# Gates of the product-key layers computed slice by slice at set paces, weight splits moved to VectorE, and a lookup of all heads at once

## The chip, the core and the metric

The kernel runs on one core of a Trainium2 chip. The metric is the device time of one launch in microseconds. The engines of the core that matter here are TensorE (PE, matrix products; its weight loads are listed as PEld), VectorE (DVE), ScalarE (ACT), GpSimd (POOL) and SyncE (SP, which issues the loads of the weights). Each engine takes its own instructions in the order in which they stand in its queue, and waits where data or a free buffer is missing.

## What is computed

The program is one inference step of a decoder of two layers for 256 prompt positions and 8 sample positions, 264 tokens in all. Each layer has a mixer and then a product-key layer ("PEER"); the change lies wholly in the second. Cut to what matters, for each token x (1024 numbers):

```
q = (x @ w_q).reshape(blk, 8, 256)                       # 8 heads
s1, s2 = q[..., :128] . k1 , q[..., 128:] . k2           # 128 scores each
v1, i1 = top_k(s1, 16); v2, i2 = top_k(s2, 16)
cand = v1[..., :, None] + v2[..., None, :]               # 16 x 16 pairs
sv, pos = top_k(cand, 16)
idx = take(i1 * 128 + i2, pos)                           # 16 experts a head
gates = softmax(sv)
h = einsum('thkd,td->thk', u_tab[idx], x)
y = einsum('thk,thkd->td', gelu(h) * gates, v_tab[idx])
```

There are 16384 experts, 128 x 128: an expert's number is i1 * 128 + i2. `u_tab` and `v_tab` have one row of 1024 numbers for each.

## The kernel before

**Prompt tokens are computed densely.** For the 256 prompt tokens the kernel doesn't gather. It multiplies all of `u_tab` with the tokens, applies gelu, multiplies by a gate that is zero for all experts but the chosen ones, and multiplies by all of `v_tab`. The 128 blocks of 128 experts that share an i1 are cut into four slices of 32 blocks (`SLICE`). `up(s)` makes `S[s]`, gelu of the products, 128 x 32 x 256, and `down(s)` multiplies `S[s]` into the output accumulators `Y`. `S` has three buffers, so the stages run up 0, up 1, up 2, down 0, up 3, down 1, down 2, down 3.

**Weights are split.** Each block of weights (128 x 1024, f32) comes by DMA into `wr` (line 49), ACT rounds it to `wh` (line 51), and VectorE or GpSimd subtracts to get the low part `wl` (line 55); three products (lines 110 to 112) then stand for one in full precision. `Stream.prep` keeps three blocks ahead of the one in use; `wh` and `wl` have four buffers. The number beside a block says which engine splits it: n means that every n-th split of the run falls to GpSimd, 0 would mean none. `peer_blocks` gives these numbers by slice. In the down stages the gated `S` is split likewise, into `ah` by ACT (line 486) and `al` by VectorE (line 488).

**Gates.** `weigh(pair)` makes the gates of two slices. For 16 tokens at a time (t0) VectorE builds one-hot rows: `ohB` over the 128 values of i2 (2048 elements) and `ohG` over the i1 of both slices (64 columns, 1024 elements), line 453; it multiplies the second by the gate's high and low part (line 470). PE multiplies the two for each token, twice (`products`, line 434, groups of 16 matmuls of 64 columns), into a buffer `pgen`, and VectorE multiplies `S` by that (`apply`, line 443).

**What sets the order.** The order is written by hand: under `manual_schedule` each engine's queue follows the code. Work beside the large products is written as generators that `yield` a cost in microseconds. `Background.spend(us)`, called after each weight block, runs the first generator in the list until that budget is used; `finish` drains one. The budget `RU` of 1.0 a block drives the top-k (`topk_head`, `topk_pairs`) during up 0 and up 1. Up 2 spends 2.4 a block on `weigh((0, 1))`, down 0 and up 3 spend 1.5 on the samples (`gathered`), down 1 spends 2.4 on `weigh((2, 3))`, down 2 nothing. `settle`, called at the end of a stage, drains a gate pass and then splits the first part of the next slice.

**Lookup.** `topk_pairs` turns positions among candidates into indices: for each half of the tokens, each side s and each of the 8 heads, it compares against `iota16` (f32), multiplies by the indices and sums over 16 entries (lines 209, 211, 213).

**Samples.** The 8 sample tokens have only 16 x 8 x 8 experts in all; `gathered` finds them, fetches their rows in 16 gathers that GpSimd issues (line 385, two buffers `grow`), and VectorE multiplies each (lines 395 and 402).

## Time and profile before

| | us |
|---|---|
| median of 3 runs | 2337.83 (2336.58 to 2338.54) |
| profiled execution, own time | 2338.07 |
| its span, first to last instruction | 2336.4 |
| PE busy | 2157.9 (92%) |
| VectorE busy | 1657.3 (71%) |
| GpSimd busy | 1008.6 (43%) |
| ScalarE busy | 945.1 (40%) |
| mean granted clock of TensorE | 0.967 of 2.4 GHz |

The two product-key layers take the stretches from 170.5 to 1089 us (layer 0) and from 1402 to 2320 us (layer 1) of the span; the first 62 and 60 us of each are the projection to q, the rest the eight stages. Matrix products on PE are pipelined: a product of 256 columns lasts about 0.28 us in the record, but the next one starts about 0.12 us after it. So the start times, and the idle time ahead of a group, tell more than PE's busy share. The releaser behind an idle time is the instruction whose end let the waiting one go.

### The profile page before, as it was taken

Reading aid. Unit: us, or ns where it says so; the run is one execution under the profiler, and the core shown is the slowest. Engines: PE = TensorE matmul, PEld = TensorE weight load, DVE = VectorE, ACT = ScalarE, POOL = GpSimd, SP = SyncE. Lnnn points to the kernel's source line nnn. Section 1 sums busy time; section 2 is a strip of 40 time slices with the busy share of each in tenths; the row PEclk is TensorE's granted clock in tenths of the full one; section 3 lists DMA queues with packets and bytes.
Section 4 is the critical chain, followed back from the end, with each engine's and each line's share of the span. In section 5 each row is a group of like instructions: output and inputs, shape, how many; then the busy total and the mean of one; then the engine's idle time right before and its main releaser. Section 6 shows DMA issues by size and latency. Waiting matters only on the chain.

```text
span 2336.4 us, 44010 instructions
## 1 busy us (share of the span) xinstructions
PE 2157.9 (92%) x17885; PEld 2031.2 (87%) x17885; DVE 1657.3 (71%) x2862; ACT 945.1 (40%) x1390; POOL 1008.6 (43%) x695
## 2 busy tenths in 40 slices
PE   8699999789999779999999999999789999779998
PEld 6379999789999779999766799999789999779997
DVE  8945699998743995445888755789998653995444
ACT  2424454224444224444543444444224444223443
POOL 6714444564534453222445334444554543553221
PEclk9799999899999889999999999999899999989999
DMA  5025554434775334553346545555434775334553
GB/s 178 26 93 176 178 181 163 136 114 149 264 244 178 109 109 154 185 177 133 132 145 220 172 142 165 187 172 170 137 109 145 260 236 187 120 105 149 183 172 106
DMA packets 111659, 371.56 MB, mean 159 GB/s; under 512 B 13865, under 2 KB 17857, under 8 KB 111456
## 3 DMA queue, kind: packets, MB, share of 16 engines
q1 hardware_dynamic: 104400, 347.73, 44.6%
q0 software_dynamic: 5728, 19.95, 2.5%
q8 instruction: 140, 2.29, 0.4%
q10 hardware_dynamic: 1328, 1.07, 0.1%
q14 instruction: 63, 0.52, 0.1%
HBM read 356.52 MB, written 12.18 MB: 158 GB/s over the span
## 4 chain that ended last, share of the span: by engine, by line
PE 55%; DVE 37%; DMA 3%; issue 2%; ACT 2%; POOL 1%; SPq 0%; ACTq 0%; DVEq 0%; POOLq 0%
PE Y L110 7%; PE Y L111 7%; PE Y L112 7%; PE pmm L110 7%; PE pmm L111 7%; PE pmm L112 7%; DVE ohG L470 7%; DVE ohG L453 4%; PE pmm L128 4%; DVE ohB L453 4%; DVE wl L55 3%; DVE tkt L209 3%; DVE S L443 3%; DVE tkt L211 2%; DVE al L488 2%
## 5 line engine op out<-in xcount | busy, mean ns | idle before, releaser
L55 POOL TENSOR_TENSOR wl<-wr,wh 128x1024 fp32r<-128x1024 f32 x303 | 759.9, 2511 | 998.4 <-ACT wh L51 937.1
L51 ACT ACTIVATE wh<-wr 128x1024 fp32r<-128x1024 f32 x579 | 610.2, 1055 | 645.1 <-PE pmm L111 144.2
L110 PE MATMUL pmm<-xh,wh 128*128 128x256 f32 (+1 forms) x2456 | 709.9, 289 | 1.9 <-ACT S L421 0.8
L112 PE MATMUL pmm<-xh,wl 128*128 128x256 f32 (+1 forms) x2456 | 697.0, 284 | 9.0 <-DVE wl L55 6.0
L111 PE MATMUL pmm<-xl,wh 128*128 128x256 f32 (+1 forms) x2456 | 698.6, 284 | 1.4 <-DVE xl L647 1.0
L110 PE MATMUL Y<-ah,wh 128*128 128x256 f32 x2048 | 592.6, 289 | 0.0
L55 DVE TENSOR_TENSOR wl<-wr,wh 128x1024 fp32r<-128x1024 f32 x276 | 364.5, 1321 | 321.2 <-ACT wh L51 320.4
L111 PE MATMUL Y<-al,wh 128*128 128x256 f32 x2048 | 586.8, 287 | 3.0 <-DVE al L488 2.9
L112 PE MATMUL Y<-ah,wl 128*128 128x256 f32 x2048 | 585.7, 286 | 0.0
L112 PEld LDWEIGHTS pmm<-xh,wl 128*128 128x128 f32 x2456 | 470.1, 191 | 10.6 <-DVE wl L55 7.2
L110 PEld LDWEIGHTS pmm<-xh,wh 128*128 128x128 f32 x2456 | 470.3, 191 | 5.0 <-ACT S L421 1.0
L111 PEld LDWEIGHTS pmm<-xl,wh 128*128 128x128 f32 x2456 | 471.2, 192 | 2.7 <-DVE xl L647 2.2
L111 PEld LDWEIGHTS Y<-al,wh 128*128 128x128 f32 x2048 | 400.3, 195 | 4.1 <-DVE al L488 4.0
L110 PEld LDWEIGHTS Y<-ah,wh 128*128 128x128 f32 x2048 | 400.4, 196 | 0.1
L112 PEld LDWEIGHTS Y<-ah,wl 128*128 128x128 f32 x2048 | 399.9, 195 | 0.0
L488 DVE TENSOR_TENSOR al<-S,ah 128x512 fp32r<-128x512 f32 x128 | 108.3, 848 | 157.1 <-ACT ah L486 157.1
L470 DVE TENSOR_TENSOR ohG<-ohG,gT 128x1024 f16<-128x1024 f16 x128 | 181.4, 1417 | 2.3
L486 ACT ACTIVATE ah<-S 128x512 fp32r<-128x512 f32 x128 | 80.5, 629 | 240.8 <-PE Y L112 236.8
L434 PE MATMUL pgen<-ohG,ohB 128*128 128x64 f16 x2048 | 87.2, 199 | 96.2 <-DVE ohG L470 82.9
L421 ACT ACTIVATE S<-pmm 128x512 f32<-128x512 f32 x128 | 76.3, 596 | 231.3 <-PE pmm L112 230.9
L434 PEld LDWEIGHTS <-ohB 128*128 128x128 f16 x2048 | 72.0, 101 | 107.9 <-DVE ohG L470 76.8
L128 PE MATMUL pmm<-x,wl 128*128 128x264 f32 x512 | 124.9, 401 | 7.9 <-DMA wl<-in_wie 6.6
(446 smaller groups left out, 2362.2 us busy)
## 6 DMA issues: line engine op xcount, KB each, us to landing
wr<-in_ut SPq DMA_DIRECT2D x256, 512.0 KB, 3.4
wr<-in_v SPq DMA_DIRECT2D x256, 512.0 KB, 3.4
wr<-in_wq SPq DMA_DIRECT2D x32, 512.0 KB, 3.5
wl<-in_wio SPq DMA_DIRECT2D x22, 512.0 KB, 3.6
wr<-in_wio SPq DMA_DIRECT2D x19, 512.0 KB, 4.8
S<-in_ssd SPq DMA_DIRECT2D x32, 256.0 KB, 2.7
out_s_ssd<-S SPq DMA_DIRECT2D x32, 256.0 KB, 3.0
wr<-in_woo SPq DMA_DIRECT2D x16, 512.0 KB, 4.0
```

The source lines that it names most:

```text
L51: k.nc.scalar.activation(hi, w, AF.Copy)
L55: eng.tensor_tensor(lo, w, hi, op=ALU.subtract)
L110: mm(out, wh, xh, start=first, stop=False, skip_group_check=True)
L111: mm(out, wh, xl, start=False, stop=False, skip_group_check=True)
L112: mm(out, wl, xh, start=False, stop=last, skip_group_check=True)
L128: self.nc.tensor.matmul(p[:, :T], wl[:, ts(i, 128)], x[:, kt], start=kt == 0, stop=kt == nk - 1, skip_group_check=True)
L421: nc.scalar.activation(S[s][:, e2:e2 + 2], p.rearrange("p (e t) -> p e t", e=2), AF.Gelu_apprx_tanh)
L434: nc.tensor.matmul(p[:, t * n:(t + 1) * n], B[:, 8 * h + t], AG[:, 8 * h + t, g], start=g == 0 and t == 0, stop=g == 1 and t == 7, skip_gr ...
L453: V.tensor_tensor(cols(out), iotah[:, i:i + n].rearrange("p (o a b) -> p o a b", o=1, b=2) .to_broadcast([128, nt, n // 2, 2]), spread(iT[ ...
L470: V.tensor_tensor(cols(AG[:, :, g]), cols(AG[:, :, 0]), spread(gT[:, g, tt], n), op=ALU.mult)
L486: nc.scalar.activation(ah, v, AF.Copy)
L488: V.tensor_sub(al, v, ah)
```

## The change

It has four parts.

First, `weigh` takes one or two slices. It is called for slice 0 alone, then for slices 1 and 2 together, then for slice 3 alone. For one slice `ohG` has 32 columns (512 elements), and a group of products is 32 matmuls of 32 columns for 16 tokens; each pass still builds `ohB` for all tokens. The pass for slice 0 is put behind the top-k in the same list, so it begins in up 1, as soon as the top-k is through; that for slices 1 and 2 runs in down 0 and up 3, that for slice 3 in down 1 and down 2. The yields follow the number of slices, and the budgets a block become 1.15 (up 0 to up 2), 1.3, 1.55, 0.9 and 0.9.

Second, `peer_blocks` gives 0 for everything but slice 0 of the up blocks and slice 3 of the down blocks, where every third split stays with GpSimd.

Third, the samples get a list of their own (`slow`) with budgets of 0.4, 0.1, 0.1, 0.25 and 0.25 a block from up 2 to down 2, and a row's gather is written behind the use of the row two before it.

Fourth, the lookup handles all 8 heads in one instruction in half precision, and sums the 16 entries by halving.

```
-RU, RQ = 1.0, 1.0
+RU, RQ = 1.15, 1.0
...
-            oh = pool.tile([128, gs, 16, 16], BF, name="tkt")
-            for g in range(g0, g0 + gs):
-                nc.vector.tensor_tensor(oh[:P, g - g0], ab[:P, s, g, :, None]..., k.iota16..., op=ALU.is_equal)
-                nc.vector.tensor_tensor(oh[:P, g - g0], oh[:P, g - g0], ff[:P, g, s, None, :]..., op=ALU.mult)
-            nc.vector.tensor_reduce(res[:P, s, g0:g0 + gs, :], oh[:P], axis=AX.X, op=ALU.add)
-            yield 0.9 * gs
+        oh = pool.tile([128, n, 16], FP16, name="ohB" if G > 1 else "tkt", bufs=2 if G > 1 else 1)
+        nc.vector.tensor_tensor(two, ab[:P, s, :, None]..., k.iota16[:P]..., op=ALU.is_equal)
+        yield 0.14 * G
+        nc.vector.tensor_tensor(four, four, ff[:P, :, s, None]..., op=ALU.mult)
+        yield 0.14 * G
+        for m in (8, 4, 2):
+            nc.vector.tensor_tensor(oh[:P, :, 0:m], oh[:P, :, 0:m], oh[:P, :, m:2 * m], op=ALU.add)
+        nc.vector.tensor_tensor(res[:P, s]..., oh[:P, :, 0], oh[:P, :, 1], op=ALU.add)
+        yield 0.16 * G
...
             rows = [row("u", 0), row("u", 1)]
+            yield 1.0
             for i in range(16):
-                if i + 2 < 16:
-                    rows.append(row("u" if i + 2 < 8 else "v", (i + 2) % 8))
...
-                yield 2.6
+                if i + 2 < 16:
+                    rows.append(row("u" if i + 2 < 8 else "v", (i + 2) % 8))
+                yield 1.5
...
                     bg.spend(us)
+                    slow.spend(us2)
...
-            n, i0 = 2 * SLICE, pair[0] * SLICE
+            n, i0 = len(pair) * SLICE, pair[0] * SLICE
+            tb = 512 // n
...
-                yield 2.3
+                yield 1.3 + 0.75 * len(pair)
...
-                yield 1.8
+                yield 1.1 * len(pair)
...
+        w = weigh((0,))
+        bg.add(w)
         up(0, RU)
         up(1, RU)
         for g in routes:
             bg.finish(g)
+        slow.add(gathered())
-        w = weigh((0, 1))
+        up(2, RU, 0.4, settle(w, 0))
+        w = weigh((1, 2))
         bg.add(w)
-        up(2, 2.4, settle(w, 0))
-        bg.add(gathered())
-        down(0, 1.5)
-        up(3, 1.5, settle(None, 1))
-        while bg.q:
-            bg.step()
-        w = weigh((2, 3))
+        down(0, 1.3, 0.1)
+        up(3, 1.55, 0.1, settle(w, 1))
+        w = weigh((3,))
         bg.add(w)
-        down(1, 2.4, settle(w, 2))
-        down(2, 0, settle(None, 3))
+        down(1, 0.9, 0.25, settle(None, 2))
+        down(2, 0.9, 0.25, settle(w, 3))
+        while slow.q:
+            slow.step()
...
-    return (ups(0, 2) + ups(1, 2) + ups(2, 1) + downs(0, 3) + ups(3, 3) + downs(1, 1) + downs(2, 3) + downs(3, 3))
+    return (ups(0, 3) + ups(1, 0) + ups(2, 0) + downs(0, 0) + ups(3, 0) + downs(1, 0) + downs(2, 0) + downs(3, 3))
```

Where instructions come to stand is shown at three places of layer 0. The line numbers are each program's own; after the change the split is still line 55, `onehot` is line 462, the multiply by the gate 479, `apply` 452, `al` 497 and the gather 391.

GpSimd from the start of up 0 on, before (`wl` is a split, `grow` a gather of the samples' rows):

```order
L548 IOTA iotah 128x128
L55 TENSOR_TENSOR wl<-wr,wh 128x1024 x66
L385 DMA grow<-in_u,idx 128x1024 x3
L55 TENSOR_TENSOR wl<-wr,wh 128x1024
L385 DMA grow<-in_u,idx 128x1024
L55 TENSOR_TENSOR wl<-wr,wh 128x1024
L385 DMA grow<-in_u,idx 128x1024 x2
L55 TENSOR_TENSOR wl<-wr,wh 128x1024
L385 DMA grow<-in_u,idx 128x1024 x2
L55 TENSOR_TENSOR wl<-wr,wh 128x1024
```

and after, up to the first load of the next layer's mixer:

```order
L558 IOTA iotah 128x128
L55 TENSOR_TENSOR wl<-wr,wh 128x1024 x10
L391 DMA grow<-in_u,idx 128x1024 x8
L391 DMA grow<-in_v,idx 128x1024 x8
L55 TENSOR_TENSOR wl<-wr,wh 128x1024 x11
L1194 DMA oddpar<-in_odd 128x154
```

Before, 66 splits stand ahead of the gathers, one or more between most of them, and 64 behind; after, 10 stand ahead of all gathers and 11 behind, 10 of these in down 3.

VectorE in the middle of a gate pass, before (up 2, slices 0 and 1; two groups of 16 tokens):

```order
L453 TENSOR_TENSOR ohB<-iotah,iT 128x2048
L443 TENSOR_TENSOR S<-S,pgen 128x32x8 x2
L453 TENSOR_TENSOR ohG<-iotah,iT 128x16x64
L443 TENSOR_TENSOR S<-S,pgen 128x32x8 x2
L470 TENSOR_TENSOR ohG<-ohG,gT 128x16x64 x2
L453 TENSOR_TENSOR ohB<-iotah,iT 128x2048
L443 TENSOR_TENSOR S<-S,pgen 128x32x8 x2
L453 TENSOR_TENSOR ohG<-iotah,iT 128x16x64
L443 TENSOR_TENSOR S<-S,pgen 128x32x8 x2
L470 TENSOR_TENSOR ohG<-ohG,gT 128x16x64 x2
```

and after (down 0, slices 1 and 2; a little over one group):

```order
L55 TENSOR_TENSOR wl<-wr,wh 128x1024
L462 TENSOR_TENSOR ohB<-iotah,iT 128x2048
L452 TENSOR_TENSOR S<-S,pgen 128x32x8 x2
L462 TENSOR_TENSOR ohG<-iotah,iT 128x16x64
L55 TENSOR_TENSOR wl<-wr,wh 128x1024 x2
L452 TENSOR_TENSOR S<-S,pgen 128x32x8 x2
L479 TENSOR_TENSOR ohG<-ohG,gT 128x16x64 x2
L55 TENSOR_TENSOR wl<-wr,wh 128x1024 x2
L462 TENSOR_TENSOR ohB<-iotah,iT 128x2048
L452 TENSOR_TENSOR S<-S,pgen 128x32x8 x2
```

The gate operations of a group are the same, but the splits of the weight blocks, which stood with GpSimd, now stand between them.

VectorE at the index lookup of the first half of the tokens, in up 0, before (three operations a head):

```order
L55 TENSOR_TENSOR wl<-wr,wh 128x1024
L209 TENSOR_TENSOR tkt<-ohG,iota_72 128x256
L211 TENSOR_TENSOR tkt<-tkt,ohG 128x256
L213 TENSOR_REDUCE ohG<-tkt 128x16
L209 TENSOR_TENSOR tkt<-ohG,iota_72 128x256
L211 TENSOR_TENSOR tkt<-tkt,ohG 128x256
L213 TENSOR_REDUCE ohG<-tkt 128x16
L55 TENSOR_TENSOR wl<-wr,wh 128x1024
```

and after (one side s of all heads, and the start of the next):

```order
L210 TENSOR_TENSOR ohB<-ohG,iota_72 128x2048
L55 TENSOR_TENSOR wl<-wr,wh 128x1024
L215 TENSOR_TENSOR ohB<-ohB,ohG 128x2048
L55 TENSOR_TENSOR wl<-wr,wh 128x1024
L218 TENSOR_TENSOR ohB<-ohB 128x128x8
L218 TENSOR_TENSOR ohB<-ohB 128x128x4
L218 TENSOR_TENSOR ohB<-ohB 128x128x2
L219 TENSOR_TENSOR ohG<-ohB 128x128
```

The 16 triples of a half of the tokens have become two runs of six operations, with splits between the large ones.

## Rows read from the trace of the kernel before

**Rows 1.** Windows by stage: us, busy time (count) by engine, granted clock, DMA share, GB/s.
```profile
232.40:324.90 92.50, 92.50 (x771) 92.50 (x771) 72.10 (x266) 45.50 (x52) 38.48 (x16) 0.98 0.54 178
324.90:419.70 94.80, 92.17 (x774) 91.36 (x773) 89.90 (x174) 43.82 (x50) 41.22 (x17) 1.00 0.52 171
419.70:564.20 144.50, 119.38 (x1286) 116.17 (x1284) 130.78 (x144) 43.25 (x50) 82.36 (x32) 0.92 0.36 122
564.20:659.80 95.60, 94.77 (x787) 94.17 (x786) 69.37 (x116) 45.04 (x53) 44.39 (x26) 1.00 0.76 256
659.80:750.60 90.80, 90.80 (x769) 90.80 (x769) 28.39 (x23) 42.88 (x49) 30.22 (x13) 1.00 0.60 195
750.60:901.50 150.90, 121.92 (x1282) 118.55 (x1281) 137.38 (x147) 42.71 (x49) 78.08 (x31) 0.90 0.34 112
901.50:993.70 92.20, 92.20 (x771) 92.20 (x769) 37.12 (x37) 42.22 (x48) 25.67 (x11) 1.00 0.57 188
...
1552.40:1649.00 96.60, 92.27 (x774) 91.45 (x774) 90.11 (x173) 43.31 (x50) 44.40 (x17) 1.00 0.51 169
1649.00:1793.20 144.20, 118.43 (x1285) 115.21 (x1284) 131.14 (x148) 43.25 (x50) 80.09 (x31) 0.92 0.37 125
1793.20:1891.90 98.70, 96.11 (x787) 95.74 (x786) 70.94 (x115) 46.64 (x54) 48.17 (x27) 0.98 0.74 248
...
1982.80:2131.90 149.10, 119.94 (x1282) 116.85 (x1282) 135.37 (x147) 42.74 (x49) 79.69 (x31) 0.91 0.35 116
```

**Rows 2.** Groups by line on PE, gate products in up 2, then down 1: busy, mean, idle before.
```profile
L434 PE MATMUL pgen<-ohG,ohB 128*128 128x64 f16 x512 | 21.4, 197 | 19.2 <-DVE ohG L470 16.5 <-DVE S L443 2.6
...
L434 PE MATMUL pgen<-ohG,ohB 128*128 128x64 f16 x512 | 21.9, 200 | 27.8 <-DVE ohG L470 23.7 <-DVE S L443 4.0
```

**Rows 3.** Timeline in up 2 (start, us), then durations of two gate lines, layer 0.
```profile
506.08 2.72 POOL L55 TENSOR_TENSOR wl<-wr,wh 128x1024 fp32r<-128x1024 f32 x1 [1.22 <-ACT wh L51]
...
507.13 2.21 DVE L453 TENSOR_TENSOR ohG<-iotah,iT 128x1024 f16<-128x1024 f16 x1
...
L470 DVE TENSOR_TENSOR ohG<-ohG,gT x64: 675/693/2882, 433.6 to 886.1; 128x1024 f16<-128x1024 f16 x64
...
L453 DVE TENSOR_TENSOR ohB<-iotah,iT x32: 1210/1218/3424, 431.8 to 878.5; 128x2048 f16<-128x2048 f16 x32
L453 DVE TENSOR_TENSOR ohG<-iotah,iT x32: 676/2220/2887, 432.9 to 880.3; 128x1024 f16<-128x1024 f16 x32
```

**Rows 4.** Durations (ns min/median/max): VectorE splits of the run; low parts and applications of layer 0.
```profile
L55 DVE TENSOR_TENSOR wl<-wr,wh x276: 1205/1226/3426, 150.8 to 2304.7; 128x1024 fp32r<-128x1024 f32 x138
...
L488 DVE TENSOR_TENSOR al<-S,ah x64: 675/693/2918, 563.7 to 1077.0; 128x512 fp32r<-128x512 f32 x64
...
L443 DVE TENSOR_TENSOR S<-S,pgen x128: 404/407/420, 438.1 to 895.0; 128x256 f32<-128x256 f32 x128
```

**Rows 5.** Timeline of PE in up 2: one group of gate products and the next matmul.
```profile
478.60 0.64 PE L434 MATMUL pgen<-ohG,ohB 128*128 128x64 f16 x16
479.08 0.37 PE L110 MATMUL pmm<-xh,wh 128*128 128x256 f32 x1
```

**Rows 6.** Durations of the three operations of the index lookup, layer 0.
```profile
L209 DVE TENSOR_TENSOR tkt<-ohG,iota x32: 412/425/2624, 308.7 to 425.0; 128x256 bf16<-128x256 f32 x32
...
L211 DVE TENSOR_TENSOR tkt<-tkt,ohG x32: 424/425/2523, 309.2 to 427.1; 128x256 bf16<-128x256 bf16 x32
...
L213 DVE TENSOR_REDUCE ohG<-tkt x32: 419/420/421, 309.7 to 429.6; 128x16 f32<-128x256 bf16 x32
```

**Rows 7.** Waits (us in total, times, longest): the whole run, then up 1 of layer 0.
```profile
DVE wl L55 <- ACT wh L51: 320.4, 187, 5.3
...
DVE tkc L395 <- DMA grow<-in_u,idx: 19.0, 6, 4.5
...
DVE wl L55 <- ACT wh L51: 1.9, 1, 1.9
...
PE pmm L112 <- DVE wl L55: 1.7, 2, 1.0
```

## What I expected, before the result

> **What bounds the kernel now.** I read the windows by stage first. [rows 1] cuts the product-key layers into stages of 32 weight blocks; the change touches seven a layer (up 0, 1, 2, down 0, up 3, down 1, 2) and not down 3. Five of the seven take 91 to 99 us with PE busy for nearly all of it. Two don't: up 2 takes 144.5 and 144.2 us, down 1 150.9 and 149.1. The floors stand in the same rows: an up stage in which PE never idles takes 90.8 (up 3), a down stage 92.2 (down 2). In the two long stages VectorE is busy 130.8 of 144.5 and 137.4 of 150.9 us, and PE's granted clock is 0.92 and 0.90. So PE is the bound everywhere but there, and there it is VectorE.
>
> [rows 2] shows how PE loses the time: it sat idle 19.2 us ahead of the gate products of up 2 and 27.8 us ahead of those of down 1, nearly all of it for the tile `ohG` of line 470. For down 1 the account closes: 27.8 idle, 15.4 of gate products (32 groups of 16 at 0.48 us, [rows 5]), and a clock 10% short over 150.9 us, 15.1: 58.3 of the 58.7 us above the floor. For up 2 it is 19.2 + 15.4 + 11.6 = 46.2 of 53.7.
>
> Next: why VectorE is so full. [rows 3] is one place: GpSimd splits a weight block from 506.08 for 2.72 us, and a gate operation of VectorE that starts at 507.13 lasts 2.21 us, ending about half a microsecond after the split does. The same form takes 0.676 at its fastest; its median in layer 0 is 2.220. Line 470 likewise: 0.693 in the median, 2.882 at worst. An operation of VectorE with two SBUF inputs that meets a GpSimd split waits it out. Down 1 at undisturbed durations ([rows 3, 4]) is 2 splits x 1.226, 16 `al` x 0.693, 16 `ohB` x 1.218, 16 one-hots x 0.676, 32 multiplies x 0.693, 64 applications x 0.407: 92.1 us. It took 137.4. The 45.3 us more, over the 31 GpSimd splits of that row, is 1.46 us a split, and a split on VectorE itself takes 1.226 [rows 4]: handing it over cost the engine that was to be relieved more than doing it.
>
> **The change, part by part.**
>
> *Splits.* By the order GpSimd does 128 splits a layer from up 0 to down 2 before and 11 after (10 of them in up 0). VectorE gets 117 more, 143 us at 1.226, and loses the stretching.
>
> *Gates.* Instead of two passes over two slices each, one in up 2 and one in down 1, there are three: slice 0 from the second half of up 1 through up 2, slices 1 and 2 over down 0 and up 3, slice 3 over down 1 and down 2. The count of `ohB` rises from 32 to 48 a layer (16 x 1.218 = 19.5 us of VectorE), and the products from 1024 to 1536, 1024 of them with 32 columns.
>
> *Lookup.* Per half of the tokens 16 triples of 0.425, 0.425 and 0.420 [rows 6] become two runs of two 2048-element operations and four shrinking adds. At 1.218 for the large ones, and sums of a fixed part of about 0.14 and half a nanosecond an element (from 0.676 and 1.218 for 1024 and 2048) for the others, a run is some 4.0 us: 16 a layer in place of 41, undisturbed.
>
> *Does VectorE fit?* Its worst stage after is down 0: 32 splits 39.2, 16 `al` 11.1, 9 `ohB` 11.0, 9 one-hots 6.1, 16 multiplies 11.1, 28 applications 11.4, two samples' rows 2.5 (bounded by a split, as wide): 92.4 us. PE's work there is 92.2 + 15 groups x 0.48 = 99.4. Counted likewise the loads are up 0 86, up 1 86, up 2 83, up 3 81, down 1 86, down 2 77, against PE work of 91, 97.5, 99.4, 99.0, 100.8, 98.9. PE should bind in all of them, with VectorE 78 to 94% full.
>
> *The sum.* (a) Up 2 and down 1 stand 53.7, 53.4, 58.7 and 56.9 us above their floors, 222.7. The products in it, 4 x 15.4 = 61.4, stay; 161.3 goes.
> (b) 512 more products a layer. With 32 columns each streams half as much as those of [rows 5] but loads the same 128x128 weights. No row has one; its step lies between half of 0.030 us (then three passes cost what two did, 0 more) and all of it (1024 x 0.030 = 30.7 more). I take the upper end, since the load is the same as in the row: +30.7.
> (c) Up 1 and down 0 stood 4.0, 5.8, 3.4 and 6.5 above their floors, 19.7 in all. [rows 7] shows that part of up 1 is PE waiting for splits late on VectorE; GpSimd leaves both stages. Between nothing and all of it I take half: -9.8.
> (d) New waits: in up 2 one product stands in the same turn as the multiplies that feed it, about 1 us; the second half of the samples' spread x now waits on ACT there, about 1; up 0 has two more heads and a lookup to do, about 1. Between 0 and 10 us over both layers, taken at +6.
>
> -161.3 + 30.7 - 9.8 + 6 = -134.4. The profiled execution took 2338.07 us (span 2336.4), the median of the runs is 2337.83; that difference is nothing here. 2337.8 - 134.4 = **2203 us**.
>
> What is costed at nothing: the samples' rows in their own queue (3.2 to 12.8 us of turns a stage), since by the order at least two blocks' work, some 6 us, lies between a gather and its use. Without that cover VectorE waits for the landing, as it did 6 times for 19.0 us in the run before, 4.5 at worst [rows 7]. Nothing else stands in GpSimd's queue behind them until the end of down 2, by the order.
>
> The Trainium skill speaks against narrow products: "TensorE: Matmul & The Clock Gate", Part 1 (section "Wait — 56ns, not 53.3ns?"), has a floor of about 25 ns from start to start however few the columns, and names 32 columns as a case. The 64-column row, 30 ns, doesn't reach that floor, and no run shows 32. By it (b) would be 20.5 instead of 30.7, and the sum 2193.
>
> **The rivals.**
>
> *Cheap products.* The load hides under half the stream, the step is 0.015: (b) is 0, and the time 2173. For it: the recorded loads last far longer than 0.03 us apiece and yet overlap. Against: nothing in the trace streams as little behind so large a load. The page's floor would exclude it; its 25 ns a product gives 2193, inside the forecast's own range.
>
> *Splits at the head of the queue, in part.* VectorE takes its work in order, and each split waits for ACT's copy `wh`, which waits for PE to release a buffer. All gates, multiplies and `al` now queue behind 32 such waits a stage. Where the wait isn't slack, it is added to the load: at 0.5 us each, 16 us a stage, up 0 rises by 11 over PE's work, down 0 by 9, up 1 by 4, down 1 by 2: 26 a layer, 2255 us. For it: VectorE waited 320.4 us in 187 such waits over the run, 1.7 each [rows 7]. Against: in up 1, where VectorE was 95% busy, 14 splits had one wait of 1.9 us. The waits belong to an engine that is early.
>
> *The same in full: slower than before.* If the 1.7 us stayed for every split, a stage would be its load plus 54 us, seven stages 972 instead of 686 a layer, and the kernel some 2770 us. The gain is used up from about 0.7 us a split that nothing fills.
>
> *The pacing doesn't do what it says.* If a gate pass isn't done when its stage ends, `settle` drains it with PE waiting, as at the end of up 2 now. At a third of each old loss this leaves 161.3/3 = 54 us: 2257. Against: by the order slice 0's last application stands six blocks ahead of the end of up 2, and the others' four.
>
> **How the numbers follow.** The forecast (PE binds, products near their row): 0.65, with 2185 to 2225 of its own. Cheap products 0.13. Head of the queue in part 0.14. Pacing off 0.03. In full 0.05, of which 0.01 falls within 0.2% of no change; 0.2%, under 5 us, is about what a measurement of this kernel can tell. The range is 2170 to 2245: it holds the forecast, most of the cheap case and half of the partial one, some 0.83. Faster 0.95, same 0.01, slower 0.04.
>
> **What would show it.** Up 2 and down 1 near 100 us with a granted clock of 1.00; no stage over 104; line 470's successor with a median and a maximum both near its minimum; PE's idle ahead of the products under 5 us a layer; groups of 32 products of 32 columns taking 0.8 to 1.0 us (0.5 would be the cheap case). VectorE's waits for `wh` should be short where it is 85% full or more. Wrong would be: PE waiting for `wl` inside blocks (head of the queue), idle at the ends of up 2, up 3 or down 2 (pacing), or a VectorE load over 100 us in any stage (my undisturbed durations).

## The result, and the profile after

The changed kernel takes 2201.68 us in the median of four runs (2200.83 to 2205.56), the kernel before beside it 2337.2 (2334.88 to 2338.54). The ratio is 0.9424, with a 95% interval of 0.9408 to 0.9441: 135.5 us less. The forecast was 2203, in a range of 2170 to 2245.

The profiled execution of the changed kernel took 2202.37 us, its span is 2200.6. The first lines are its busy times and the shares of the chain of waits that ended last, from the page.

```profile
PE 2142.2 (97%) x18909; PEld 2022.1 (92%) x18909; DVE 1626.7 (74%) x3029; ACT 944.1 (43%) x1390; POOL 414.1 (19%) x460
...
PE 86%; DVE 10%; ACT 1%; DMA 1%; issue 1%; POOL 1%; SPq 0%; ACTq 0%; DVEq 0%; POOLq 0%
```

TensorE is busy 97% of the span in place of 92%, VectorE has 31 us less to do although it took over 117 splits a layer, and GpSimd's 1008.6 us have become 414.1. In the chain before, TensorE had 55% and VectorE 37%.

Next the windows by stage, which answer [rows 1]: up 0, up 1, up 2, down 0, up 3, down 1 and down 2 of layer 0, then up 2 of layer 1 (columns: us, busy time and count by engine, granted clock, DMA share, GB/s).

```profile
232.30:323.20 90.90, 90.90 (x770) 90.90 (x770) 81.13 (x283) 45.52 (x52) 24.56 (x10) 1.00 0.58 182
323.20:421.00 97.80, 97.80 (x999) 97.37 (x998) 79.55 (x156) 44.94 (x53) 0.00 (x0) 1.00 0.55 177
421.00:526.00 105.00, 101.27 (x1081) 100.55 (x1076) 75.67 (x144) 45.35 (x54) 5.00 (x4) 1.00 0.57 178
526.00:626.50 100.50, 100.50 (x1010) 99.71 (x1010) 84.67 (x114) 42.19 (x48) 3.13 (x2) 1.00 0.57 182
626.50:726.80 100.30, 100.30 (x1043) 99.55 (x1041) 75.33 (x103) 41.70 (x48) 2.71 (x2) 1.00 0.57 178
726.80:827.10 100.30, 100.30 (x1059) 99.77 (x1057) 79.96 (x102) 43.44 (x52) 5.34 (x5) 1.00 0.63 196
827.10:925.60 98.50, 98.50 (x999) 98.20 (x996) 72.91 (x88) 41.59 (x48) 6.46 (x4) 1.00 0.59 186
...
1582.20:1688.70 106.50, 102.77 (x1079) 102.05 (x1075) 75.62 (x144) 45.32 (x53) 5.00 (x4) 0.98 0.56 177
```

Up 2 and down 1 have come down from 144.5 and 150.9 us to 105.0 and 100.3, and up 3 and down 2 have risen by 9.5 and 6.3, since they now hold products too. In six of layer 0's seven stages TensorE never sits idle, and the granted clock is 1.00. Over both layers the eight stages take 1579.5 us in place of 1715.1: 135.6 less, which is the whole result. The rest of the kernel didn't move.

Last, durations of VectorE's operations in layer 0 (ns, least/median/most; of lines 479 and 462 the smaller form is that of one slice), and VectorE's largest wait over the run. They answer [rows 3, 4, 7].

```profile
L479 DVE TENSOR_TENSOR ohG<-ohG,gT x96: 417/425/694, 363.7 to 899.9; 128x512 f16<-128x512 f16 x64, 128x1024 f16<-128x1024 f16 x32
L462 DVE TENSOR_TENSOR ohG<-iotah,iT x48: 417/421/692, 361.1 to 893.3; 128x512 f16<-128x512 f16 x32, 128x1024 f16<-128x1024 f16 x16
...
L497 DVE TENSOR_TENSOR al<-S,ah x64: 683/693/694, 525.4 to 1008.9; 128x512 fp32r<-128x512 f32 x64
```

```profile
DVE wl L55 <- ACT wh L51: 320.9, 276, 6.1
```

The tails of 2.2 to 2.9 us are gone: no multiply, one-hot or `al` lasts longer than its form does undisturbed. The wait of splits for ACT's copy is, in total, what it was (320.4 before), though VectorE does far more of them.

### The profile page after: what moved, and what is told of

Same layout as the page of the kernel before. It is cut to its first block, busy times and chain, and to the rows that moved or that the text cites. A ratio compares the mean times of both kernels' runs of the same rounds, so it can differ in the third digit from the quotient of the medians.

```text
span 2200.6 us, 45912 instructions
## 1 busy us (share of the span) xinstructions
PE 2142.2 (97%) x18909; PEld 2022.1 (92%) x18909; DVE 1626.7 (74%) x3029; ACT 944.1 (43%) x1390; POOL 414.1 (19%) x460
## 4 chain that ended last, share of the span: by engine, by line
PE 86%; DVE 10%; ACT 1%; DMA 1%; issue 1%; POOL 1%; SPq 0%; ACTq 0%; DVEq 0%; POOLq 0%
PE pmm L110 13%; PE pmm L111 12%; PE pmm L112 12%; PE Y L110 11%; PE Y L111 11%; PE Y L112 11%; PE pmm L128 4%; PE pgen L443 4%; PE pys L1485 1%; DVE rot L882 1%; DVE wl L55 1%; DVE pl L901 1%; PE pgen L638 1%; PE pgen L620 1%; DVE cy L1306 1%
## 5 line engine op out<-in xcount | busy, mean ns | idle before, releaser
L55 DVE TENSOR_TENSOR wl<-wr,wh 128x1024 fp32r<-128x1024 f32 x511 | 629.4, 1232 | 325.1 <-ACT wh L51 320.9
L110 PE MATMUL Y<-ah,wh 128*128 128x256 f32 x2048 | 585.3, 286 | 0.0
L111 PEld LDWEIGHTS Y<-al,wh 128*128 128x128 f32 x2048 | 392.7, 192 | 0.7
L112 PEld LDWEIGHTS Y<-ah,wl 128*128 128x128 f32 x2048 | 392.7, 192 | 0.0
L110 PEld LDWEIGHTS Y<-ah,wh 128*128 128x128 f32 x2048 | 392.5, 192 | 0.1
L55 POOL TENSOR_TENSOR wl<-wr,wh 128x1024 fp32r<-128x1024 f32 x68 | 165.1, 2428 | 458.6 <-ACT wh L51 423.8
L497 DVE TENSOR_TENSOR al<-S,ah 128x512 fp32r<-128x512 f32 x128 | 88.4, 690 | 98.1 <-ACT ah L495 98.1
L391 POOL DMA_INDIRECT grow<-in_u,idx x16 | 21.7, 1355 | 735.5 <-DVE tkc L400 359.0
L128 PEld LDWEIGHTS pmm<-x,wl 128*128 128x128 f32 x512 | 100.5, 200 | 27.6 <-issue 8.5
L462 DVE TENSOR_TENSOR ohB<-iotah,iT 128x2048 f16<-128x2048 f16 x96 | 117.0, 1219 | 0.0
```

The costliest lines, as they stand in the source:

```text
L55: eng.tensor_tensor(lo, w, hi, op=ALU.subtract)
L110: mm(out, wh, xh, start=first, stop=False, skip_group_check=True)
L111: mm(out, wh, xl, start=False, stop=False, skip_group_check=True)
L112: mm(out, wl, xh, start=False, stop=last, skip_group_check=True)
L128: self.nc.tensor.matmul(p[:, :T], wl[:, ts(i, 128)], x[:, kt], start=kt == 0, stop=kt == nk - 1, skip_group_check=True)
L462: V.tensor_tensor(cols(out), iotah[:, i:i + n].rearrange("p (o a b) -> p o a b", o=1, b=2) .to_broadcast([128, nt, n // 2, 2]), spread(iT[ ...
```

## Which part of the change brought it

### The splits alone

The kernel before, with nothing but the new table of who splits:

```
-    return (ups(0, 2) + ups(1, 2) + ups(2, 1) + downs(0, 3) + ups(3, 3) + downs(1, 1) + downs(2, 3) + downs(3, 3))
+    return (ups(0, 3) + ups(1, 0) + ups(2, 0) + downs(0, 0) + ups(3, 0) + downs(1, 0) + downs(2, 0) + downs(3, 3))
```

Expected:

> The kernel before, with nothing changed but the numbers of peer_blocks: up 1, 2, 3 and down 0, 1, 2 split on VectorE alone. Theory (the gate operations were stretched by GpSimd's splits): VectorE's undisturbed work is 115 us in up 2 and 129 in down 1, so these stages fall from 144 and 150 to about 119 and 132, all else stays: about 2250 us. Rival (the 131 and 137 us that VectorE was busy there are the operations' own, and a split more is just more work): 168 and 174 us, about 2430.

Measured: 2215.26 us (2213.3 to 2217.07), ratio 0.9485 (0.9467 to 0.9503), 120 us less than before. That is 35 us better than the 2250 I had for it: the one line brings nearly nine tenths of the result. Some 22 of the 35 us lie in up 2 and down 1, which take 116.1 and 123.8 us in both layers where I had 119 and 132, and 13 in up 1 and down 0, of which I had thought that they would stay: they take 91.2 and 94.8 us in both layers in place of 94.8 and 96.6, 95.6 and 98.7. The windows of up 2 and down 1 of this kernel, and the durations of its one-hot rows in down 1:

```profile
416.60:532.70 116.10, 109.56 (x1285) 107.57 (x1284) 109.87 (x170) 42.18 (x49) 0.00 (x0) 1.00 0.44 146
...
718.40:842.20 123.80, 113.69 (x1282) 111.56 (x1282) 116.86 (x177) 42.75 (x49) 0.00 (x0) 0.97 0.42 137
```

```profile
L470 DVE TENSOR_TENSOR ohG<-ohG,gT x32: 682/691/695, 723.7 to 828.5; 128x1024 f16<-128x1024 f16 x32
L453 DVE TENSOR_TENSOR ohG<-iotah,iT x16: 682/685/686, 723.0 to 824.8; 128x1024 f16<-128x1024 f16 x16
```

Against [rows 1], VectorE has 26 and 30 operations more in the two stages and is busy 20.9 and 20.5 us less. All 32 multiplies in down 1 now last 0.68 to 0.70 us. That is the reading of [rows 3] made into an experiment: taking work from GpSimd onto the full engine relieved the full engine.

### Everything but the splits

The changed kernel with the old table:

```
-    return (ups(0, 3) + ups(1, 0) + ups(2, 0) + downs(0, 0) + ups(3, 0) + downs(1, 0) + downs(2, 0) + downs(3, 3))
+    return (ups(0, 2) + ups(1, 2) + ups(2, 1) + downs(0, 3) + ups(3, 3) + downs(1, 1) + downs(2, 3) + downs(3, 3))
```

> The kernel after, with the numbers of peer_blocks of before: 128 splits a layer with GpSimd from up 0 to down 2. Theory (two causes, and spreading the gates would do most of it alone): each of the splits stretches VectorE by 1.5 us in place of its own 1.2, its load rises by 7 us at most a stage (up 2: 76 to 83) and stays under PE's 100; some products wait one stretched operation, about 2 us: 2205 to 2235 us. Rival (most of the gain comes from GpSimd's leaving): half of the 135 us is lost, about 2270 or more.

Measured: 2278.52 us (2275.62 to 2282.66), ratio 0.9762 (0.974 to 0.9784). My 2205 to 2235 fell, and the rival's 2270 and more held: slicing, lookup and queue together bring 57 us as long as GpSimd splits. Up 1 takes 105.4 and 103.5 us, up 2 109.9 and 110.5, and down 1 123.7 and 126.1. The last was unexpected, since VectorE has less to do there than in the changed kernel, where 80 us of work fit into 100.3. The group of gate products on TensorE in down 1 of layer 0, the durations of the multiplies there (ns, least/median/most), and then the timeline of VectorE and GpSimd (start us, us, idle before in brackets):

```profile
L443 PE MATMUL pgen<-ohG,ohB 128*128 128x32 f16 x286 | 8.7, 178 | 16.5 <-DVE ohG L479 16.5
```

```profile
L479 DVE TENSOR_TENSOR ohG<-ohG,gT x18: 410/2253/7780, 750.3 to 862.5; 128x512 f16<-128x512 f16 x18
```

```profile
746.35 3.46 DVE L400 SCALAR_TENSOR_TENSOR tkc<-grow,x 128x1024 bf16<-128x1024 f32 x1
...
750.09 1.17 POOL L391 DMA_INDIRECT grow<-in_v,idx  x1 [1.36 <-DVE tkc L400]
...
750.34 8.22 DVE L479 TENSOR_TENSOR ohG<-ohG,gT 128x512 f16<-128x512 f16 x2
751.27 7.00 POOL L55 TENSOR_TENSOR wl<-wr,wh 128x1024 fp32r<-128x1024 f32 x3
```

A gather in GpSimd's queue has to wait 1.36 us until VectorE has done with the buffer, and starts at 750.09. Behind it three splits run without a gap from 751.27 for 7.00 us. The second of the two multiplies on VectorE, 0.42 us undisturbed, starts ahead of them and ends after the third: it is the one of 7.78 us. Before the change the longest operation of VectorE in the run was 3.83 us; here six are longer than 3.5, all of them multiplies in down 1, three a layer, and each starts while GpSimd issues a gather behind which three splits run in one piece. So a gather in GpSimd's queue turns three short blockades into one long one, and gate products wait for the multiply: 16.5 us in this stage, 13.6 of them behind those three multiplies. The clock is 0.94, by my estimate another 7.4 us of 123.7. Together, 23.9, that comes to the 23.4 us by which the stage is longer than in the changed kernel. Down 1, over both layers, has 49 of the 77 us that this kernel takes more than the changed one. Up 1 is 7.6 and 5.3 us longer and up 2 4.9 and 4.0, and in these too TensorE waits for multiplies.

### The same without gathers among the splits

If that account holds, down 1 must come down when no gather stands in it, with all 31 GpSimd splits left:

```
-        down(1, 0.9, 0.25, settle(None, 2))
-        down(2, 0.9, 0.25, settle(w, 3))
+        down(1, 0.9, 0.0, settle(None, 2))
+        down(2, 0.9, 0.5, settle(w, 3))
```

> The kernel of e2 (old splits) with the samples' budget 0 in down 1 and 0.5 in down 2, so that no gather stands among GpSimd's 30 splits of down 1. Theory (a gather waits for VectorE, splits pile up behind it and then run back to back, and VectorE's next operation of two SBUF inputs waits for all of them, up to 7.8 us): down 1 falls from 124 us to about 110, as up 2 has with as many splits: 2248 to 2258. Rival (the number of splits alone does it): down 1 stays at 124, 2275 to 2282.

Measured: 2240.96 us (2236.62 to 2242.31), ratio 0.9591 (0.9562 to 0.9619); better than I had expected, and the rival fell. Its window of down 1, the durations of the multiplies, and the group of products:

```profile
740.70:846.40 105.70, 100.86 (x1058) 99.80 (x1057) 93.58 (x64) 43.33 (x51) 80.32 (x31) 1.00 0.53 163
```

```profile
L479 DVE TENSOR_TENSOR ohG<-ohG,gT x18: 412/2475/2614, 749.4 to 844.4; 128x512 f16<-128x512 f16 x18
```

```profile
L443 PE MATMUL pgen<-ohG,ohB 128*128 128x32 f16 x288 | 8.7, 176 | 3.6 <-DVE ohG L479 3.6
```

The multiplies are still stretched, 2.475 us in the median, but none is over 2.614, and the stage takes 105.7 us in place of 123.7, with 3.6 us of idle ahead of the products in place of 16.5. The lower budget takes the samples' own work on VectorE out of the stage as well, 10.5 us in layer 0, so this run alone doesn't part the two; that it was the piled-up splits rests on the three long multiplies above, behind which 13.6 of the 16.5 us were lost.

So two things are to be kept apart. A single split stretches a multiply sixfold; splits that pile up behind a waiting gather stretch it to 7.78 us. The first isn't free either. This kernel takes 39 us more than the changed one: down 1 is still 5.4 us longer in each layer, and up 1, which has 18 splits on GpSimd and no gather, takes 104.9 and 104.8 us in place of 97.8 and 98.2, with 4.1 us of idle ahead of products for the multiply.

### The lookup, alone and beside the splits

The kernel before with only the new lookup, and then with the new table of splits as well:

```
-            for g in range(g0, g0 + gs):
...
-            nc.vector.tensor_reduce(res[:P, s, g0:g0 + gs, :], oh[:P], axis=AX.X, op=ALU.add)
...
+        oh = pool.tile([128, n, 16], FP16, name="ohB" if G > 1 else "tkt", bufs=2 if G > 1 else 1)
...
+        nc.vector.tensor_tensor(four, four, ff[:P, :, s, None].to_broadcast([P, G, 16, 16]), op=ALU.mult)
...
+        for m in (8, 4, 2):
+            nc.vector.tensor_tensor(oh[:P, :, 0:m], oh[:P, :, 0:m], oh[:P, :, m:2 * m], op=ALU.add)
```

> The kernel before, with the lookup of all heads at once alone. Theory: up 0 and up 1 are PE's, so what VectorE is spared there is worth little; what goes is the end of the top-k that PE waits for at the start of up 2 (6 us a layer) and the lookups that VectorE still does in up 2 (some 10): 12 to 30 us in all, 2307 to 2325 us. Rival (hidden beside PE altogether): within 5 us of 2337.

> The kernel before with both the new numbers of peer_blocks and the lookup of all heads at once; the gates stay in two passes of two slices. Theory (with GpSimd out, up 2 and down 1 are VectorE's at undisturbed durations, 116 and 124 us in e1, and the lookup was beside PE already): 2205 to 2215, so that slicing the gates is worth some 10 us. Rival (the two gains add): 2215 - 25 = 2190, and slicing costs.

Measured: 2310.41 us (2308.24 to 2311.7), ratio 0.9893 (0.9875 to 0.9912), for the first, 25 us less than before; 2210.05 (2208.05 to 2211.81), ratio 0.9478 (0.9462 to 0.9494), for the second. Both came in the bands of their theories, and the rival that the two gains add, 2190, fell. Nearly all of the lookup's 25 us lie in up 2, at whose start the last heads' lookup still had to be done. The window of up 2, lookup alone:

```profile
417.60:551.10 133.50, 115.33 (x1283) 112.37 (x1281) 114.60 (x125) 42.19 (x49) 79.74 (x31) 0.95 0.39 128
```

It is 11 us shorter than in [rows 1], and VectorE is busy 16 less; down 1, where there is no lookup, stays at 149.9. The trace of the kernel before has TensorE waiting 4.4 us in that stage for the tile of line 213 and 1.6 for that of line 217, which is most of the 7.5 us that the prediction's account of up 2 left open. Once the splits have left GpSimd, the lookup adds little: 2215.26 and 2210.05 come from different comparisons, and their ratios' intervals overlap. The two don't add up: both relieve VectorE in up 2, and beside the new table the lookup takes 3 us of VectorE's busy time there (109.9 to 106.9) where alone it took 16.

What is left for slicing, paces and the samples' queue, which no run parts from each other, is the step from 2210.05 to 2201.68: 8 us by the medians, 13 by the ratios (0.9478 to 0.9424, intervals apart). They take up 2 from 114.8 to 105.0 and down 1 from 123.5 to 100.3 us, but pay for it with 512 products more a layer and with some 6 us more in each of up 1, down 0 and down 2 and 9 in up 3.

## What bounds the kernel now

### Half of the gate products

The loop over the two parts of the gate runs once: the products of the low part are left out, everything else stays.

```
-                    for g in range(2):
+                    for g in range(1):
...
-                                         start=g == 0 and t == 0, stop=g == 1 and t == tb - 1, skip_group_check=True)
+                                         start=g == 0 and t == 0, stop=g == 0 and t == tb - 1, skip_group_check=True)
```

> The kernel after without the gate products of the low part: PE does half of them, VectorE does all it did (the output lacks the gate's low part). Theory (PE binds every stage): half of the 82.5 us that the products take in the trace of the kernel after goes, 41 us: 2158 to 2168. Rival (VectorE or its waits set the pace): 2190 to 2202.

Measured: 2160.09 us (2159.8 to 2160.27), ratio 0.925 (0.9224 to 0.9276): 41.6 us less than the changed kernel. By the rows, all groups of products take 82.6 us in both layers (64 groups of 32 products of 32 columns at 0.81, 64 of 16 products of 64 columns at 0.48), and half of that is 41.3. What was taken from TensorE's queue came out of the time, to within a microsecond. The rival that VectorE still sets the pace, 2190 to 2202, fell.

### Less and more work on VectorE

One kernel leaves out the multiply by the gate's low part (the product uses the high part twice), one writes `ohB` twice, one three times. The three edits, one after the other:

```
-                        nc.tensor.matmul(p[:, t * n:(t + 1) * n], B[:, tb * h + t], AG[:, tb * h + t, g],
+                        nc.tensor.matmul(p[:, t * n:(t + 1) * n], B[:, tb * h + t], AG[:, tb * h + t, 0],
...
-                for g in (1, 0):
+                for g in (0,):
...
+                onehot(B, 1, 0, 128, tt)
...
+                onehot(B, 1, 0, 128, tt)
+                onehot(B, 1, 0, 128, tt)
```

> The kernel after without VectorE's multiply by the gate's low part; PE does the same number of products, with the high part twice (the output has the gate's high part doubled). 48 operations, 25 us of VectorE, fall away in each layer. Theory (PE binds): only up 2's two waits behind multiplies shrink: 2194 to 2202. Rival (VectorE sets the pace): 49 us less, about 2153.

> The kernel after, with the one-hot rows ohB written twice by VectorE: 48 operations of 1.22 us more a layer, 58 us, 9 to 11 a stage from up 1 to down 2. Theory (PE binds, VectorE has room: it is busy 73 to 85 of 98 to 106 us): 2202 to 2215 us. Rival (VectorE's order sets the pace, since each of its splits waits for ACT): all of it shows, 2300 to 2320.

> The kernel after with ohB written three times, 117 us of VectorE more a layer: its load becomes about 96 us in up 1, 96 in up 2, 104 in down 0, 92 in up 3, 101 in down 1, 89 in down 2. Theory (VectorE sets the pace a little before it is full, at some 95%): 2225 to 2265. Rival (it can be filled to the last, and only down 0 and down 1 pass PE's 100): 2212 to 2222.

Measured: 2195.91 us (2194.97 to 2196.86), ratio 0.9405 (0.9378 to 0.9431), with less work; 2208.49 (2207.58 to 2212.24), ratio 0.9461 (0.9442 to 0.948), with 58 us more a layer; 2262.54 (2259.8 to 2262.89), ratio 0.9697 (0.9681 to 0.9713), with 117 more. The first two came in the bands of the theory that TensorE binds, and the rivals that VectorE sets the pace, 2153 and 2300 to 2320, fell. The third came at the upper end of its theory's band, that VectorE sets the pace a little before it is full; the rival that it can be filled to the last, 2212 to 2222, fell. Less work is 5.8 us below the changed kernel by the medians, but the intervals of the two ratios overlap; in the stages 4.7 us went, 4.2 of them in up 2 (103.6 us in both layers). Windows with `ohB` written twice (up 2, down 0), then three times (up 1, up 2, down 0, up 3, down 1):

```profile
420.30:529.70 109.40, 103.85 (x1078) 103.06 (x1075) 86.12 (x153) 45.33 (x53) 5.02 (x4) 0.97 0.53 171
529.70:630.20 100.50, 100.50 (x1010) 99.72 (x1009) 94.19 (x123) 42.24 (x48) 2.94 (x2) 1.00 0.58 182
```

```profile
323.10:422.40 99.30, 98.04 (x999) 97.37 (x998) 95.99 (x170) 45.05 (x53) 0.00 (x0) 1.00 0.55 173
422.40:540.20 117.80, 104.42 (x1080) 103.50 (x1077) 96.97 (x162) 45.31 (x54) 5.00 (x4) 0.96 0.51 160
540.20:644.30 104.10, 101.90 (x1011) 100.22 (x1010) 101.11 (x127) 42.41 (x48) 2.84 (x2) 1.00 0.51 171
644.30:751.50 107.20, 102.49 (x1043) 101.12 (x1041) 96.04 (x123) 41.87 (x48) 3.63 (x2) 0.98 0.54 171
751.50:855.10 103.60, 101.00 (x1058) 99.88 (x1057) 99.42 (x120) 43.86 (x52) 5.76 (x5) 1.00 0.58 189
```

Down 0 with 94.2 us of VectorE work takes 100.5 us, to the digit what it took with 84.7. With 101.1, which is more than TensorE's 99.4, it takes 104.1. Up 3 loses more with less: 107.2 in place of 100.3, with VectorE at 96.0 us, since TensorE waits 4.7 us there for VectorE's gate operations, 3.4 of them for the application of an earlier product, and the clock is 0.98. So the load of a stage alone doesn't say where the limit is. Up 2 shows it best: it grows by 4.4 us (1.8 in layer 1) already with VectorE at 86 us, and to 117.8 with 97, where TensorE waits 12.7 us for the multiply. The products of slice 0 stand right behind the multiplies that feed them, so what VectorE does just before them is waited for.

### Up 2, the one stage with idle time

The timeline of the changed kernel in up 2 of layer 0 shows its waits:

```profile
462.36 0.88 DVE L479 TENSOR_TENSOR ohG<-ohG,gT 128x512 f16<-128x512 f16 x2
463.15 1.22 DVE L55 TENSOR_TENSOR wl<-wr,wh 128x1024 fp32r<-128x1024 f32 x1
463.29 0.95 PE L443 MATMUL pgen<-ohG,ohB 128*128 128x32 f16 x32 [1.60 <-DVE ohG L479]
```

```profile
490.24 0.93 PE L443 MATMUL pgen<-ohG,ohB 128*128 128x32 f16 x31 [1.45 <-DVE ohG L479]
...
501.61 0.60 ACT L383 ACTIVATE x<-pgen 128x512 f32<-128x512 f32 x1 [3.69 <-PE pgen L381]
502.26 0.97 PEld L381 LDWEIGHTS pgen<-ident,grow 128*128 128x128 f32 x8 [0.88 <-ACT x L383]
502.26 1.16 PE L381 MATMUL pgen<-ident,grow 128*128 128x128 f32 x8 [0.69 <-ACT x L383]
```

Two groups of products wait 1.60 and 1.45 us for the multiply, and the products that spread the samples' x wait 0.69 for ACT: 3.7 us. The spreading itself, 16 products of which the last eight are shown, takes 1.8. It was in down 0 before.

I tried to move part of that with the samples' budgets alone:

```
-        up(2, RU, 0.4, settle(w, 0))
+        up(2, RU, 0.25, settle(w, 0))
...
-        down(0, 1.3, 0.1)
-        up(3, 1.55, 0.1, settle(w, 1))
+        down(0, 1.3, 0.15)
+        up(3, 1.55, 0.15, settle(w, 1))
...
-        down(1, 0.9, 0.25, settle(None, 2))
-        down(2, 0.9, 0.25, settle(w, 3))
+        down(1, 0.9, 0.3, settle(None, 2))
+        down(2, 0.9, 0.3, settle(w, 3))
```

> The kernel after with the samples' budget in up 2 lowered from 0.4 to 0.25 a block and raised by 0.05 in the four stages behind. Theory (up 2's 14 to 16 us above PE's bare blocks hold some 4 us a layer of products that wait for multiplies, since the samples' top-k comes between): 2194 to 2200. Rival (those waits come from the pass itself): no change, 2200 to 2203.

Measured: 2199.51 us (2198.38 to 2201.33), ratio 0.9419 (0.9397 to 0.9442). The median lies in the theory's band, but the single runs reach into the rival's. Up 2 fell to 102.6 and 101.1 us, but down 0 rose to 103.3 in both layers, since half of the spreading and its wait for ACT went there. The gain is not told from none.

### Two versions with fewer products

If TensorE binds, one product of 64 columns in place of two of 32 should pay. In the passes over one slice, this kernel multiplies the high and the low part side by side; ACT copies the high half out of the buffer, VectorE adds the low half and applies the sum.

```
-            tb = 512 // n
+            tb = 8
...
+                    if len(pair) == 1:
+                        nc.tensor.matmul(p[:, t * 64:(t + 1) * 64], B[:, tb * h + t],
+                                         AG[:, tb * h + t].rearrange("p g n -> p (g n)"),
+                                         start=t == 0, stop=t == tb - 1, skip_group_check=True)
...
+                    nc.scalar.activation(m, w[:, 0], AF.Copy)
+                    V.tensor_tensor(w[:, 1], m, w[:, 1], op=ALU.add)
+                    o = S[pair[0]][:, :, t0:t0 + tb]
+                    V.tensor_tensor(o, o, w[:, 1], op=ALU.mult)
```

> The kernel after with one product of 64 columns (high and low part side by side) in place of two of 32 in the passes over one slice; ACT copies the high half out, VectorE adds the low one and applies the sum, 2 x 0.42 us for 8 tokens in place of 0.68 for 16. Theory (a product of 32 columns costs 25 ns, one of 64 costs 30, and PE binds): 16 tokens cost 0.48 us of PE in place of 0.81, 21 us less in all: 2178 to 2188. Rivals: the price goes by columns, no gain, 2200 to 2203; or VectorE's 16 us more a pass show, 2215 and above.

Measured: 2193.24 us (2191.77 to 2193.97), ratio 0.9402 (0.9386 to 0.9417). This missed the 2178 to 2188 of my theory, and neither rival's band holds it. Windows of up 2, down 1 and down 2:

```profile
419.20:524.40 105.20, 99.72 (x940) 98.11 (x937) 85.56 (x176) 51.15 (x74) 5.28 (x4) 1.00 0.56 178
725.30:822.90 97.60, 97.60 (x907) 96.73 (x905) 85.50 (x124) 47.18 (x67) 5.76 (x5) 1.00 0.60 200
822.90:919.80 96.90, 96.90 (x894) 96.26 (x891) 80.82 (x114) 46.48 (x64) 5.23 (x4) 1.00 0.58 190
```

The theory asks for 0.33 us a group, 3.0 us in down 1 and 2.3 in up 1 and in down 2. Down 1 and down 2 gave 2.7 and 1.6 us, up 1 0.6, since TensorE waits 1.45 us there for the tile `gT`. Up 2 gave nothing: TensorE has less to do there, 99.7 us busy in place of 101.3, but waits 5.5 us in place of 3.7, since VectorE got 10 us more work ahead of products that follow it closely. By the medians it is 8 us below the changed kernel, and the sum over the stages says the same (9 us), but the intervals of the two ratios overlap. Of the versions that keep the low part it has the lowest time.

The last kernel leaves out the gate's low part altogether, multiplies and products, on the samples' budgets tried above:

```
-                    for g in range(2):
-                        nc.tensor.matmul(p[:, t * n:(t + 1) * n], B[:, tb * h + t], AG[:, tb * h + t, g],
+                    nc.tensor.matmul(p[:, t * n:(t + 1) * n], B[:, tb * h + t], AG[:, tb * h + t, 0],
...
-                for g in (1, 0):
+                for g in (0,):
```

> The kernel after without the gate's low part altogether, neither multiply nor product (the gate is left in half precision), and with the samples' budgets of e7. Theory: e5's 41 us, and a few of up 2's waits: 2148 to 2158. Rival (the waits are elsewhere): as e5, 2160.

Measured: 2155.68 us (2152.06 to 2156.29), ratio 0.9243 (0.9228 to 0.9258), inside its band; up 2 takes 96.7 us in both layers. It shows what the gate's low part costs, by the medians 44 us (against the kernel on the same budgets) to 46, and is no replacement, since the gate then has half precision only.

## Why the prediction was right

The reading held: VectorE bound two stages, GpSimd's splits filled it, and with the splits gone and the gates spread TensorE sets the time of all stages but for 3.7 us of waits in each up 2. The sum, 2203, is 1.3 us off, and that it comes so near is luck: (b) was 9.6 too high, (c) took 4.7 too little away, (d) was 13.2 too low, and these cancel. By the windows after, with (d) as what the others leave of the whole:

| term | predicted | measured |
|---|---|---|
| (a) the excess of up 2 and down 1, less their products | -161.3 | -161.3, by definition; see below |
| (b) products added | +30.7 | +21.1 |
| (c) up 1 and down 0 | -9.8 | -14.5 |
| (d) what new stands above TensorE's work | +6 | +19.2 |
| sum | -134.4 | -135.5 |

**(b) was mis-sized by the choice of its end.** I took 30 ns for a product of 32 columns, the row for 64. The first line is a group of 32 products in up 2, the second the weight product behind it (start us, us):

```profile
426.77 0.97 PE L443 MATMUL pgen<-ohG,ohB 128*128 128x32 f16 x32
427.58 0.37 PE L110 MATMUL pmm<-xh,wh 128*128 128x256 f32 x1
```

That is 0.81 us from start to start, 25 ns a product; 64 columns still take 0.48 us for 16, 30 ns. So it is neither half nor all of it. The Trainium skill, "TensorE: Matmul & The Clock Gate", Part 1 (section "Wait — 56ns, not 53.3ns?"), has a floor of about 25 ns however few the columns; the trace agrees, here with a weight load for each product. By it (b) was 20.5, against 21.1 measured.

**(c) went further, because work left.** Up 1 stands 1.3 and 1.7 us above its floor and its seven groups of products, down 0 1.1 and 1.1. I took half of the 19.7 us; 14.5 went. But the spreading of the samples' x left down 0 for up 2, so part of this gain is paid back in (d).

**(d) is the step that failed,** outside its own bound of 10. Most of it is up 2, which stands 6.9 and 8.4 us above its floor and products. I had the mechanisms, products in the same turn as their multiplies and a wait for ACT, but took 1 us apiece where the waits are 1.60, 1.45 and 0.69, and I left out that the spreading's own 1.8 us come along. In layer 1 the clock of 0.98 takes up to 2 us more. The up 0 that I expected to lose a microsecond is at its floor, and in layer 0, where it took 92.5 us before, it gave back 1.6.

Another part of (d) should never have been in (a). After a group of gate products the first weight product is followed later than usual:

```profile
537.66 0.64 PE L443 MATMUL pgen<-ohG,ohB 128*128 128x64 f16 x16
538.13 0.36 PE L110 MATMUL Y<-ah,wh 128*128 128x256 f32 x1
538.34 0.28 PE L111 MATMUL Y<-al,wh 128*128 128x256 f32 x1
538.45 0.28 PE L112 MATMUL Y<-ah,wl 128*128 128x256 f32 x1
```

The step from 538.13 to 538.34 is 0.20 us in the median of the 126 such places that the trace holds whole, where 0.12 is usual, and it was so before (0.20, from 479.08 to 479.28). With 64 groups a layer, before and after, this is by estimate 0.08 x 128 = some 10 us that the change couldn't remove. I counted it in (a) as loss that goes. Why the step is longer no run shows. Three stages show it bare: up 3, down 1 and down 2 stand 1.3, 0.8 and 0.6 us above their sums, with 17, 9 and 7 groups.

**VectorE's loads** came out lower than counted: 81, 80, 76, 85, 75, 80 and 73 us in place of 86, 86, 83, 92, 81, 86 and 77. Durations overlap where operations stand back to back, as three starts in up 2 show:

```profile
425.97 1.21 DVE L55 TENSOR_TENSOR wl<-wr,wh 128x1024 fp32r<-128x1024 f32 x1
427.09 1.22 DVE L462 TENSOR_TENSOR ohB<-iotah,iT 128x2048 f16<-128x2048 f16 x1
428.23 0.42 DVE L462 TENSOR_TENSOR ohG<-iotah,iT 128x512 f16<-128x512 f16 x1
```

A split of 1.21 us is followed after 1.12, an `ohB` of 1.22 after 1.14. The sum of durations was a bound on the safe side, and the error had no part in the time of the changed kernel; in that of the splits alone, where VectorE still bound two stages, it was part of the 35 us.

**The rivals.** Cheap products is ruled out by the 25 ns. The queue's head, in part or in full, didn't come: VectorE waited 320.9 us for `wh`, the same total as before, in 276 waits in place of 187, and TensorE's idle time ahead of the products with `wl` is 2.9 us over the whole run (line 112 with `pmm`) and none in the down stages. The waits belong to an engine that is early, as [rows 7] suggested: 58 us more work a layer on VectorE cost 7 us in all by the medians. The pacing does what it says: TensorE has no idle time at the ends of up 2, up 3 and down 2. Of what was to show it, two lines failed, both in up 2: no stage was to be over 104 us, and it takes 105.0 and 106.5, in layer 1 at a clock of 0.98 in place of 1.00. Idle time ahead of the products is 3.0 us a layer, under the 5 named. The samples' rows, costed at nothing, cost VectorE nothing: there is no wait of it for a gather after the change.

**What the prediction didn't price** is the share of each part. It described the splits rightly, 1.46 us of cost for 1.226 of relief, and yet when I had to give numbers for the parts I gave the splits 88 us and they brought 120, and I gave the rest over 100 and it brought 57. Together the parts bring 135.5, less than 120 + 57, because they cure, for the most part, the same two stages.

## What to carry to other kernels

Before work is handed to a second engine as relief, compare what the relieved engine's own operations last beside it and without it: here each handed-over split cost VectorE more than it saved (1.46 us against 1.226), and taking them back brought 120 of some 2336 us in one line. When two stages are cured down to the bound engine's work, what is left to forecast are that engine's small steps, the price of a narrow product and of each change between kinds of products, times their count; read those start to start, and don't put them among the losses that go. And an instruction that may wait (here a gather) in the queue of an engine that disturbs another can turn several short blockades into a long one, so look at the longest operation of the disturbed engine, not only at the median.

## What the hardware showed that I had not expected

- An operation of VectorE with two SBUF inputs didn't get in between splits that GpSimd ran back to back: 0.42 us became 7.78 with three of them. The application of a gate, which reads one operand from PSUM, kept its 404 to 420 ns beside splits [rows 4]. The Trainium skill, "GPSIMD Engine Reference", section "1. Specifications", says that the two engines contend for SBUF when VectorE has two SBUF inputs; the trace agrees.
- How full VectorE may be is a matter of what stands behind its operations. Down 0 bore 94.2 us of it in 100.5 without a loss, and lost 3.6 us with 101.1 us where TensorE has 99.4. Up 3 lost 6.9 us with 96.0, and up 2, where products stand right behind their multiplies, 4.4 and 1.8 us with 86.
- A product of 32 columns costs 25 ns from start to start beside 30 for 64, each with a weight load of its own.
